# A hybrid decoder layer on one core: token sums moved to VectorE, first weight sums made earlier, weight slots moved, and another product order in the down projection

## The chip, the core and the metric

One core of a Trainium2 chip runs the whole layer in one launch. The metric is the device time of that launch in microseconds. The engines are named as in the profile: PE (TensorE), DVE (VectorE), ACT (ScalarE), POOL (GpSimd), and SP, which here only issues DMAs. POOL issues a few DMAs too. Every engine runs its instructions in the order in which they stand, and an instruction that waits holds up all behind it on that engine.

## The reference, cut to what matters

```python
u  = rmsnorm(x, attn_pre_norm)                    # x: 1024 tokens x 1024, float32
mix = concat(latent attention, HGRN2 recurrence)  # from one input projection
h  = x + rmsnorm(mix @ w_out, attn_post_norm)
z  = rmsnorm(h, ffn_pre_norm)
ff = silu(z @ w_gate) * (z @ w_up)                # width 2816
out = h + rmsnorm(ff @ w_down, ffn_post_norm)
```

## The kernel before, in words

The tokens lie in 8 blocks of 128. Three stages matter here: w_out (blocks y, some 540 to 618 us in the profile), gate and up (618 to 1073), and down (1073 to the end).

**Float32 by three products.** Each operand is split into a high part (a cast to fp32r on ACT) and a low part (a subtraction on DVE). A product is high x high, high x low and low x high, accumulated in PSUM.

**Seven products in place of eight.** Gate, up and down use a Strassen form (Winograd's variant): both operands are cut into 2 x 2 blocks, sums of blocks are made, and seven block products p1 to p7 replace eight. Of the tokens, b11, b21 and b22 are blocks and t1 to t4 are sums (`t1`, `t2` per token block at L965 to L971, `t3` at L1159, `t4` at L1164). Of each weight pair m (11 pairs of gate and of up columns, so m = 0 to 21, even for gate, odd for up) `w_sums` (L1002) makes three sums and L1019 a fourth. Of the down weights `wd_sum` (L1087) makes four sums on POOL, which go to `wb_d` in HBM. `ff_out` (L1068) makes four sums of the result of a pair on POOL and stores seven blocks to `fa_d`; down reads both back.

**w_out.** For each block t the mixed values are split (`mh` on ACT, `ml` on DVE L831), PE runs 48 matmuls, then z(t-2) is transposed (`z_t`, `zt` at L962), and `post_y`, `post_z` make h and z on DVE and ACT. The block's x comes by a DMA on SP into one of two buffers (L927), free once block t-2 has been transposed. DVE needs x at L939 and writes the normed block at L948. Up to block 6 a scheduler sets the order, from there on the order is that of the program text (`manual_schedule`, L1116).

**Gate and up.** The table `seq` (L984 to L987) lists 154 pairs (m, p), each a product of 12 matmuls of 128x512 at L1041. `w_prep` (L1009) splits a weight block into one of eight slots, six products ahead: slots 0 to 3 are the tile `wvg` (pool `gen`, on the right side of SBUF), slots 4 to 7 the tile `wvx` (pool `fqp`, on the left). The weights come through the tile `w4`; `w_load` is issued when the last block of the pair two before has been split. `post` (L1044) reads PSUM. The first 20 or so products stand in an order of their own, mixed with the last two token blocks' transposes (L1181 to L1228). For m below 4 the weight sums are on POOL, and so are the token sums t3 and t4.

**Down.** 77 steps (p, i), seven products of 11 steps; a step is one 512 KB load into one of four buffers `dgen` (`d_load`, L1237), one split (`d_prep`, L1242: a cast on ACT, a subtraction on DVE of 128x1024) and 12 matmuls (L1352), 3 for each of four token blocks j. The last steps of each product are run block by block (three steps, six in the last product), so that the results of block 0 leave PSUM (`d_post`, L1321) while the others are still at work. In the last product p3 each block's result goes through a square with a sum (ACT), a root (`rms_s`) and the output (`half`, `out_t`).

Of the kernel before, what the change touches and what calls it, by code (L numbers as in the profile page):

```python
# [85 lines left out]
def hymba_block(ctx: ExitStack, tc: tile.TileContext, a: dict, out: bass.AP):  # L86
# [53 lines left out]
    def rms_s(ss, name):  # L140
# [861 lines left out]
    def w_sums(m, E_):  # L1002
        a11, a12, a21, a22 = (ws_[m][:, j, :] for j in range(4))
        s1 = ffq["s1", m % 2]
        E_.tensor_tensor(s1, a21, a22, op=ALU.add)
        E_.tensor_tensor(a21, a11, a21, op=ALU.subtract)
        E_.tensor_tensor(a11, s1, a11, op=ALU.subtract)  # L1007

    def w_prep(n):  # L1009
# [57 lines left out]

    def ff_out(i):  # L1068
# [31 lines left out]
    for t in range(NT - 1):  # L1100
# [47 lines left out]
    wvx = fqp.tile([P, 2 * (NS - 4), 512], F32R, name="wvx")  # L1148
    wv += [wvx[:, 2 * j:2 * j + 2, :] for j in range(NS - 4)]
# [35 lines left out]
    for m in range(2):  # L1185
        w_sums(m, G)
# [61 lines left out]
    dgen, d_slots = None, [wvg[:, 4:8], wvx[:, 0:4], wvx[:, 4:8]]  # L1248

    for n in range(9, len(seq)):  # L1250
# [213 lines left out]
```

## Time and profile before

| | us |
|---|---|
| median of 3 runs | 1303.67 (1303.16 to 1304.64) |
| the profiled execution's own time | 1302.41 |
| its span | 1299.90 |
| PE busy | 1243.6 |
| DVE busy | 893.2 |
| ACT busy | 559.1 |
| POOL busy | 344.0 |

The profiled execution is one run of the same program; what lies around its span is 2.51 us. PE is busy for 96% of the span, so the stretches in which it is not, and those in which its granted clock (PEclk; 1.00 is 2.4 GHz, 0.50 is 1.2 GHz) is low, are what to look for. Matmuls overlap: one lasts 390 ns, but the next starts some 230 ns after it.

### The profile page before, as it was taken

How to read it: one execution, taken by the hardware profiler on the slowest of the kernel's cores; microseconds unless marked ns; L12 is line 12 of the kernel's file. 1: busy time of each engine (PE TensorE's matmuls, PEld its weight loads, DVE VectorE, ACT ScalarE, POOL GpSimd, SP SyncE). 2: the span in 40 equal slices, each digit the busy share in tenths (PEclk: the TensorE clock that was granted, in tenths of full speed). 3: DMA queues.
4: the chain of work that ended last, by engine and by line, in shares of the span. 5: the costliest groups of instructions: out<-in, count | busy, mean ns of one | idle time of the engine just before them, and what ended most of it. 6: DMA issues, size and time to landing. Idle time of an engine off the chain costs nothing.

```text
span 1299.9 us, 18112 instructions
## 1 busy us (share of the span) xinstructions
PE 1243.6 (96%) x6436; PEld 1034.1 (80%) x6436; DVE 893.2 (69%) x1786; ACT 559.1 (43%) x1202; POOL 344.0 (26%) x401
## 2 busy tenths in 40 slices
PE   8999999999999998999789999999999998999996
PEld 6987787898788887888567888888888887888885
DVE  6837657543888989677977777667677664555578
ACT  6424334336867766444432222333222333444352
POOL 1015433411232334000565523233323221000000
PEclk8999999999999998999889999999999998999998
DMA  8330100101000002225025453444353447755765
GB/s 281 108 114 18 49 27 10 35 5 65 19 7 8 33 1 81 87 101 186 33 82 182 173 186 120 156 170 164 135 187 130 154 161 256 242 183 180 257 200 189
DMA packets 61386, 155.20 MB, mean 119 GB/s; under 512 B 7153, under 2 KB 8561, under 8 KB 61297
## 3 DMA queue, kind: packets, MB, share of 16 engines
q1 hardware_dynamic: 60192, 150.38, 33.7%
q0 software_dynamic: 1104, 3.67, 0.8%
q8 instruction: 51, 0.84, 0.3%
q14 instruction: 39, 0.31, 0.1%
HBM read 112.87 MB, written 41.16 MB: 118 GB/s over the span
## 4 chain that ended last, share of the span: by engine, by line
PE 74%; DVE 13%; ACT 4%; issue 3%; DMA 3%; POOL 2%; SPq 0%; DVEq 0%; ACTq 0%; POOLq 0%
PE g_B L1041 8%; PE g_E L1041 8%; PE g_A L1041 8%; PE dy_B L1352 5%; PE g_C L1041 4%; PE dy_A L1352 4%; PE dy_C L1352 2%; PE dy_E L1352 2%; PE ao L768 2%; PE lv L437 2%; PE y L96 2%; PE y L95 2%; PE y L94 2%; PE lat_ps L96 1%; DVE s L737 1%
## 5 line engine op out<-in xcount | busy, mean ns | idle before, releaser
L1245 DVE TENSOR_TENSOR dhl<-dgen,dhl 128x1024 fp32r<-128x1024 f32 x74 | 89.3, 1223 | 73.8 <-ACT dhl L1244 73.5
L1244 ACT CAST dhl<-dgen 128x1024 fp32r<-128x1024 f32 x74 | 76.5, 1050 | 99.4 <-PE dy_B L1352 32.0
L1022 ACT CAST wvx<-w 128x512 fp32r<-128x512 f32 x64 | 39.0, 617 | 105.7 <-DVE w L1007 46.1
L1023 DVE TENSOR_TENSOR wvg<-w,wvg 128x512 fp32r<-128x512 f32 x64 | 58.8, 920 | 31.3 <-ACT wvg L1022 31.2
L1022 ACT CAST wvg<-w 128x512 fp32r<-128x512 f32 x64 | 39.1, 617 | 94.2 <-DVE w L1019 40.6
L1023 DVE TENSOR_TENSOR wvx<-w,wvx 128x512 fp32r<-128x512 f32 x64 | 53.1, 830 | 33.4 <-ACT wvx L1022 33.3
L738 ACT ACTIVATE pe<-s,nm 128x128 f32<-128x128 f32 (+3 forms) x64 | 47.7, 746 | 40.0 <-DVE nm L737 24.0
L1073 POOL TENSOR_TENSOR fq_p<-fq_u,fq_p 128x512 f32<-128x512 f32 x11 | 19.0, 1731 | 173.3 <-DVE fq_u L1066 173.3
L1352 PE MATMUL dy_B<-dhl 128*128 128x512 f32 x264 | 60.2, 389 | 0.0
L1352 PE MATMUL dy_E<-dhl 128*128 128x512 f32 x264 | 60.2, 389 | 0.0
L1352 PE MATMUL dy_A<-dhl 128*128 128x512 f32 x228 | 55.5, 405 | 3.3 <-ACT dhl L1244 2.7
L1352 PEld LDWEIGHTS dy_E<-dhl 128*128 128x128 f32 x264 | 49.5, 188 | 10.3
L1352 PEld LDWEIGHTS dy_B<-dhl 128*128 128x128 f32 x264 | 49.5, 188 | 10.3
L1313 POOL DMA_DIRECT2D out_dram<-ot x8 | 4.4, 548 | 195.5 <-DVE ot L1312 195.1
L1352 PEld LDWEIGHTS dy_A<-dhl 128*128 128x128 f32 x228 | 44.7, 197 | 13.7 <-ACT dhl L1244 3.1
L759 DVE TENSOR_TENSOR ptl<-pt,pth 128x512 fp32r<-128x512 f32 (+2 forms) x96 | 49.9, 552 | 4.4 <-ACT pth L758 3.6
L755 PE MATMUL pt<-cc,pe 128*128 128x128 f32 x288 | 44.9, 277 | 6.2 <-DVE oT L774 5.5
L737 DVE CUSTOM_DVE_ANT_0 s<-mbuf,s 128x128 f32<-128x128 bf16 (+6 forms) x56 | 41.9, 749 | 7.2 <-PE s L728 6.3
L758 ACT CAST pth<-pt 128x512 fp32r<-128x512 f32 (+2 forms) x96 | 43.6, 483 | 6.1 <-PE pt L755 6.0
L458 POOL TENSOR_TENSOR kk<-kk,tt 128x128 f32<-128x128 f32 (+1 forms) x88 | 40.8, 493 | 14.1 <-PE lv L453 14.1
L755 PEld LDWEIGHTS pt<-cc,pe 128*128 128x128 f32 x288 | 34.1, 142 | 12.2 <-DVE oT L774 7.2
L1054 DVE TENSOR_TENSOR fq_u<-g_B,fq_p 128x512 f32<-128x512 f32 x22 | 15.2, 691 | 34.5 <-PE g_B L1041 23.0
(475 smaller groups left out, 3906.3 us busy)
## 6 DMA issues: line engine op xcount, KB each, us to landing
dgen<-fa_p SPq DMA_DIRECT2D x77, 256.0 KB, 3.8
w<-in_w_gate_dram SPq DMA_DIRECT2D x22, 512.0 KB, 4.2
w<-in_w_up_dram SPq DMA_DIRECT2D x22, 512.0 KB, 5.1
wdr<-in_w_down_dram SPq DMA_DIRECT2D x22, 512.0 KB, 6.3
wb_d<-wdr SPq DMA_DIRECT2D x22, 512.0 KB, 6.4
fa_p<-fq_u SPq DMA_DIRECT2D x44, 256.0 KB, 2.0
dgen<-wb_d SPq DMA_DIRECT2D x44, 256.0 KB, 4.2
dgen<-in_w_down_dram SPq DMA_DIRECT2D x33, 256.0 KB, 4.1
```

The costliest lines, as they stand in the source:

```text
L458: E_.tensor_tensor(v_, v_, pick(tg, 2 * n * j + to_, t_[c_:]), op=ALU.mult)
L737: V.tensor_tensor_reduce(sv, mv, sv, op0=ALU.add, op1=ALU.min, scale=1.0, scalar=3e38, accum_out=nm)
L738: A.activation(pv, sv, AF.Exp, bias=nm, scale=-1.0, accum_out=zz[:, NT * h + qb:NT * h + qb + 1])
L755: T.transpose(tps[:, j, :], pe[:, (k0 + j) * P:(k0 + j + 1) * P], ident)
L758: A.copy(th[o], tps[:, 0:n, :])
L759: V.tensor_tensor(tl[o], tps[:, 0:n, :], f32(th[o]), op=ALU.subtract)
L1022: A.copy(wh, src)
L1023: V.tensor_tensor(wl, src, f32(wh), op=ALU.subtract)
L1041: T.matmul(o, l_[:, k_], r_[:, k, :], start=first and k == 0 and i == 0, stop=k == 3 and i == 2, skip_group_check=True)
L1244: A.copy(hl[:, 0, :], raw)
L1245: V.tensor_tensor(hl[:, 1, :], raw, f32(hl[:, 0, :]), op=ALU.subtract)
L1352: T.matmul(dq[bank[p]][j], hl[:, lh, j_], hl[:, rh, 512:1024], start=first and x_ == 0, stop=i == NP - 1 and x_ == 2, skip_group_check=True)
```

## The change

- The token sums t3 and t4 run on DVE; t3 in one piece after the last block, t4 in six steps after products 9 to 14.
- The weight sums of m = 0 to 3 are made on POOL during w_out, from block 0 to 3 on, one m for each (`w_pre`), and stored to `ws_d` in HBM. `w_load` reads them back. The blocks that p1 and p2 need come through `w_early` for all four.
- The eight weight slots are two tiles `wva`, `wvb` in `gen` on the right side; `w4` has a pool of its own on the left, takes its first loads after w_out, and serves down's loads as well (so `dgen` is `w4`).
- The order of p3 and p4 for m = 0, 1, the places of the last two blocks' work, of `wd_load`, `wd_sum`, `wd_store` and of `ff_out`'s last four stores (`ff_store`) are others.
- Down's products run as p1, p2, p6, p5, p3, p7, p4 in place of p1, p6, p2, p5, p7, p4, p3; the last product's last eight steps run block by block in place of six. Loads 4 to 6 of down are issued in the last gate and up products. A part of the root's sum is made earlier.

```diff
-DN_END = 6
+DN_END = 8
+T4_AT = 9
+PRE = 4
+DN_PRODUCTS = ("p1", "p2", "p6", "p5", "p3", "p7", "p4")
...
-    seq += [(m, p) for p in ("p5", "p7") for m in range(2)]
-    seq += [(m, p) for m in range(2) for p in ("p3", "p4")]
+    seq += [(m, p) for p in ("p5", "p7", "p3", "p4") for m in range(2)]
...
+            SP.dma_start(wq[:, j, :], ws_d[m, j] if m < PRE else w_of[m % 2][m // 2 + NP * j])
+        if m < PRE:
+            SP.dma_start(ffq["s1", m % 2], w_of[m % 2][m // 2 + NP][:, 512:1024])
...
+    def w_pre(m):
+        pre_ = [wr.tile([P, D], F32, name=f"wp{m}_{j}", tag="wr") for j in range(2)]
+        for j in range(2):
+            SP.dma_start(pre_[j], w_of[m % 2][m // 2 + NP * j])
+        (a11, a12), (a21, a22) = ([x_[:, d_] for d_ in halves] for x_ in pre_)
+        G.tensor_tensor(a22, a21, a22, op=ALU.add)
+        G.tensor_tensor(a21, a11, a21, op=ALU.subtract)
+        G.tensor_tensor(a11, a22, a11, op=ALU.subtract)
+        G.tensor_tensor(a12, a12, a11, op=ALU.subtract)
+        for j in range(2):
+            SP.dma_start(ws_d[m, j], pre_[j])
...
-        if p == "p6" and m > 1:
-            w_sums(m, G if m < 4 else V)
-        if p == "p3":
+        if p == "p6" and m >= PRE:
+            w_sums(m)
+        if p == "p3" and m >= PRE:
             V.tensor_tensor(a12, a12, a11, op=ALU.subtract)
...
         post_y(t)
         post_z(t)
+        if t < PRE:
+            w_pre(t)
...
-    w4[0] = gen.tile([P, 4, 1024], F32, name="w4", tag="gen")
-    wvg = gen.tile([P, 8, 512], F32R, name="wvg", tag="gen")
+    for x_ in "ab":
+        wg_ = gen.tile([P, 8, 512], F32R, name=f"wv{x_}", tag="gen")
...
-    wvx = fqp.tile([P, 2 * (NS - 4), 512], F32R, name="wvx")
...
+    def t3_sum():
+            V.tensor_tensor(zr["t1"], zr["t1"] if i else zr["t2"], f32(x_), op=ALU.subtract)
+    def t4_step(x):
+            V.tensor_tensor(t4r[j], f32(zv["b21"][i][:, j_, :]), t4r[j] if i else zr["t2"][:, j_, :],
+                            op=ALU.add if i else ALU.subtract)
...
-    for m in range(2):
-        w_sums(m, G)
     product(0)
...
             d_prep(e_ // 2, d_slots[e_ // 2].rearrange("p (x a) c -> p x (a c)", x=2))
+            d_load(e_ // 2 + 4)
...
+        if first:
+            V.tensor_tensor(ssy[:, o_:o_ + 1], ssy[:, o_:o_ + 1], eps, op=ALU.add)
...
-            (SP if t < 4 else G).dma_start(out[t][:, d_], ot[:, d_])
+            (G if t < 4 else SP).dma_start(out[t][:, d_], ot[:, d_])
```

Three places show how instructions moved.

SP's queue in w_out, around the loads of x for blocks 4 and 5. Before (`xr_6554`, `xr_6657` are x of blocks 4 and 5, `h_3` to `h_5` stores of h):

```order
L940 DMA h_d<-h_3_6453 128x1024
L927 DMA xr_6554<-in_x_dram 128x1024
L940 DMA h_d<-h_4_6556 128x1024
L927 DMA xr_6657<-in_x_dram 128x1024
L940 DMA h_d<-h_5_6659 128x1024
```

After (`xr_6595`, `xr_6698` are x of blocks 4 and 5; `wp` a pair whose sums POOL makes, `ws_d` its store, `we` an early load):

```order
L1007 DMA wp_0_6514<-in_w_up_dram 128x1024
L947 DMA h_d<-h_3_6484 128x1024
L1007 DMA wp_1_6515<-in_w_up_dram 128x1024
L931 DMA xr_6595<-in_x_dram 128x1024
L1014 DMA ws_d<-wp_1_6515 128x1024
L1014 DMA ws_d<-wp_0_6514 128x1024
L1020 DMA we_6846<-in_w_gate_dram 128x1024
L947 DMA h_d<-h_4_6597 128x1024
L1020 DMA we_6848<-in_w_up_dram 128x1024
L931 DMA xr_6698<-in_x_dram 128x1024
```

The x of block 5 now stands behind two stores that wait for POOL's sums of m = 3, and behind two loads that wait for these stores.

DVE from the last block's t1 split to the t3 split in gate and up. Before (`wvg`, `wvx` the weight slots, `zr_t` the raw token sums):

```order
L953 TENSOR_TENSOR z_t1l<-zr_t_6164,z_t1h 128x4x128
L1023 TENSOR_TENSOR wvx<-w_6803,wvx 128x512
L1066 TENSOR_TENSOR fq_c_6905<-g_A,fq_c_6905 128x512
L1023 TENSOR_TENSOR wvg<-we_7056,wvg 128x512
L1023 TENSOR_TENSOR wvg<-w_6803,wvg 128x512
L1023 TENSOR_TENSOR wvg<-s_0_6900,wvg 128x512
L1052 TENSOR_TENSOR fq_u_6903<-g_B,fq_p_6902 128x512
L953 TENSOR_TENSOR z_t3l<-zr_t_6164,z_t3h 128x2048
```

After:

```order
L960 TENSOR_TENSOR z_t1l<-zr_t_6165,z_t1h 128x4x128
L1047 TENSOR_TENSOR wvb<-w_6947,wvb 128x512
L1090 TENSOR_TENSOR fq_c_6962<-g_A,fq_c_6962 128x512
L1047 TENSOR_TENSOR wva<-we_6911,wva 128x512
L1203 TENSOR_TENSOR zr_t_6165<-zr_t_6166,z_b11h 128x2048
L1203 TENSOR_TENSOR zr_t_6165<-zr_t_6165,z_b11l 128x2048
L1047 TENSOR_TENSOR wva<-w_6947,wva 128x512
L960 TENSOR_TENSOR z_t3l<-zr_t_6165,z_t3h 128x2048
L1047 TENSOR_TENSOR wva<-w_6947,wva 128x512
L1076 TENSOR_TENSOR fq_u_6960<-g_B,fq_p_6959 128x512
```

The two t3 sums stand on DVE ahead of the splits for products 9 and 10; before, POOL made them.

SP's queue at the end of gate and up. Before (`fa_p` from `fq`: stores of a pair's result; `dgen` loads of down's steps, each in two halves, here step 4's):

```order
L1078 DMA fa_p_74<-fq_p_6906 128x512
L1078 DMA fa_p_75<-fq_u_6903 128x512
L1078 DMA fa_p_72<-fq_u_6908 128x512
L1078 DMA fa_p_77<-fq_u_6907 128x512
L1239 DMA dgen<-fa_p_71 128x512
L1240 DMA dgen<-in_w_down_dram 128x512
L1294 DMA fpost<-in_ffn_post_dram 128x1024
```

After (`w_6947` is `w4`; the first four rows load steps 5 and 6, step 4's stand earlier; `wb_d` from `wdr` stores down's weight sums):

```order
L1274 DMA w_6947<-fa_p_71 128x512
L1275 DMA w_6947<-in_w_down_dram 128x512
L1274 DMA w_6947<-fa_p_71 128x512
L1275 DMA w_6947<-in_w_down_dram 128x512
L1126 DMA wb_d<-wdr_0_9781 128x1024
L1126 DMA wb_d<-wdr_1_9782 128x1024
L1098 DMA fa_p_71<-fq_c_6962 128x512
L1098 DMA fa_p_73<-fq_u_6961 128x512
L1098 DMA fa_p_76<-fq_p_6959 128x512
L1108 DMA fa_p_74<-fq_p_6963 128x512
L1108 DMA fa_p_75<-fq_u_6960 128x512
L1108 DMA fa_p_72<-fq_u_6965 128x512
```

Loads 4 to 6 moved ahead of the last pair's stores; the first load behind them, after one of `fpost`, is now step 7's.

## Rows read from the trace of the kernel before

**Rows 1.** The page's first part: busy time of each engine.
```profile
PE 1243.6 (96%) x6436; PEld 1034.1 (80%) x6436; DVE 893.2 (69%) x1786; ACT 559.1 (43%) x1202; POOL 344.0 (26%) x401
```
**Rows 2.** Stretches: length, each engine's busy time (instructions), PEclk, DMA share, GB/s.
```profile
618.30:692.80 74.50, 60.77 (x234) 47.62 (x233) 60.65 (x68) 27.29 (x44) 45.63 (x23) 0.86 0.17 57
...
1073.40:1110.30 36.90, 33.61 (x134) 26.85 (x133) 17.23 (x15) 14.05 (x15) 6.03 (x4) 0.91 0.79 270
...
625.00:630.00 5.00, 4.43 (x12) 3.26 (x11) 4.56 (x12) 1.12 (x5) 1.00 (x1) 0.50 0.00 2
```
**Rows 3.** PE's longest wait from 605 to 720 us: total, times, longest.
```profile
PE g_E L1041 <- DVE fq_p L1055: 5.6, 1, 5.6
```
**Rows 4.** PE in order of time: start, length, [idle before].
```profile
618.23 0.39 PE L1041 MATMUL g_A<-z_b11h,wvg 128*128 128x512 f32 x1
...
623.56 1.97 PE L962 MATMUL zt<-cc,xr 128*128 128x128 f32 x8 [2.42 <-DVE xr L948]
...
630.75 0.39 PE L1041 MATMUL g_A<-z_b21h,wvg 128*128 128x512 f32 x1
...
692.78 0.40 PE L1041 MATMUL g_B<-z_t2h,wvg 128*128 128x512 f32 x1
...
705.70 0.39 PE L1041 MATMUL g_C<-z_t4h,wvx 128*128 128x512 f32 x1
```
**Rows 5.** POOL and DVE in order of time, in the same stretch.
```profile
615.78 1.74 POOL L1005 TENSOR_TENSOR s<-w 128x512 f32<-128x512 f32 x1 [93.18 <-DVE rr_z L135]
...
616.29 1.25 DVE L136 TENSOR_TENSOR rt_z<-rr_z 128x1 f32<-128x1 f32 x1
...
619.24 0.68 DVE L968 TENSOR_TENSOR zr_t<-zt,z_b11h 128x512 f32<-128x512 f32 x1
...
637.22 1.75 DVE L953 TENSOR_TENSOR z_t1l<-zr_t,z_t1h 128x1536 fp32r<-128x1536 f32 x1
...
639.60 3.48 DVE L968 TENSOR_TENSOR zr_t<-zr_t,z_b11l 128x512 f32<-128x512 f32 x1
```
**Rows 6.** w_out: DVE and SP by time; DMA issues, median us to landing.
```profile
538.55 2.35 DVE L157 TENSOR_TENSOR wol<-wo_r,woh 128x1024 fp32r<-128x1024 f32 x2
...
582.79 0.33 SPq L927 DMA_DIRECT2D xr<-in_x_dram  x1
...
594.67 0.33 SPq L927 DMA_DIRECT2D xr<-in_x_dram  x1
...
606.09 0.69 DVE L831 TENSOR_TENSOR ml<-mixa,mh 128x512 fp32r<-128x512 f32 x1 [1.82 <-PE zt L962]
...
h_d<-h SPq DMA_DIRECT2D x6, 512.0 KB, 2.6
...
w<-in_w_gate_dram SPq DMA_DIRECT2D x2, 512.0 KB, 4.1
```
**Rows 7.** PE: first matmuls of four products, two with each slot tile.
```profile
1051.34 0.39 PE L1041 MATMUL g_E<-z_b22h,wvg 128*128 128x512 f32 x1
...
1054.06 0.39 PE L1041 MATMUL g_A<-z_b11h,wvg 128*128 128x512 f32 x1
...
1059.55 0.39 PE L1041 MATMUL g_A<-z_b21h,wvx 128*128 128x512 f32 x1
...
1062.35 0.39 PE L1041 MATMUL g_E<-z_t1h,wvx 128*128 128x512 f32 x1
```
**Rows 8.** Start of down: SP by time; then the chain of waits.
```profile
1081.74 0.38 SPq L1239 DMA_DIRECT2D dgen<-fa_p  x1
...
1110.28 29.92 PE dy_B L1352 x132
```
**Rows 9.** End of the span: PE and DVE by time; a stretch as in rows 2.
```profile
1259.72 30.08 PE L1352 MATMUL dy_E<-dhl 128*128 128x512 f32 x132
...
1292.31 0.68 DVE L1342 TENSOR_TENSOR d_u<-dy_E,d_u 128x512 f32<-128x512 f32 x1
...
1284.00:1288.00 4.00, 4.00 (x19) 3.34 (x18) 3.56 (x11) 1.02 (x3) 0.00 (x0) 1.00 0.48 188
```

More of the change, by code (lines that the diff above doesn't have):

```diff
@@ L1066, in post @@
                 V.tensor_tensor(sl, o if p == "p2" else own(done), sl, op=ALU.mult)
+    wd_at = {**{2 * i + 3: i for i in range(NP - 2)}, 2 * NP - 2: NP - 2, 2 * NP - 1: NP - 1}
     def ff_out(i):
@@ L1117, in hymba_block @@
     ms.__enter__()
-    w4[0] = gen.tile([P, 4, 1024], F32, name="w4", tag="gen")
-    wvg = gen.tile([P, 8, 512], F32R, name="wvg", tag="gen")
-    wv += [wvg[:, 2 * j:2 * j + 2, :] for j in range(4)]
-    for m in range(2):
-        w_load(m)
+    for x_ in "ab":
+        wg_ = gen.tile([P, 8, 512], F32R, name=f"wv{x_}", tag="gen")
+        wv += [wg_[:, 2 * j:2 * j + 2, :] for j in range(4)]
+        wvt.append(wg_)
+    w_early(0)
+    w_early(1)
+    w_prep(0)
+    w_prep(2)
+    w_early(2)
+    w_prep(1)
+    w_prep(4)
+    x_get(last)
     mix_mm(last, order, (0,))
     post_y(last, (0,))
-    w_early(2)
-    for n in range(4):
-        w_prep(n)
     z_t(last - 2, sm)
+    w_prep(3)
+    w_prep(5)
+    w_early(3)
     mix_mm(last, order, (1,))
@@ L1134, in hymba_block @@
     ps.close()
+    w4_st = ExitStack()
+    w4p = pool(w4_st, "w4p")
+    w4[0] = w4p.tile([P, 4, 1024], F32, name="w4")
     f_st = ExitStack()
@@ L1139, in hymba_block @@
         ffq["s1", i] = fqp.tile([P, 512], F32, name=f"s1_{i}")
+    for m in range(2):
+        w_load(m)
     def ff_tiles(p_, par):
@@ L1228, in hymba_block @@
     w_prep(14)
-    steps = [(p, i) for p in PRODUCTS for i in range(NP)]
+    steps = [(p, i) for p in DN_PRODUCTS for i in range(NP)]
     dv = {}
@@ L1246, in d_prep @@
         dv[n] = hl
-    dgen, d_slots = None, [wvg[:, 4:8], wvx[:, 0:4], wvx[:, 4:8]]
+    dgen, d_slots = w4[0], [wvt[0][:, 4:8], wvt[1][:, 0:4], wvt[1][:, 4:8]]
     for n in range(9, len(seq)):
@@ L1294, in hymba_block, with half @@
     SP.dma_start(fpost, a["ffn_post"].partition_broadcast(P))
-    p1_, u2_, u3_ = (dp.tile([P, 4, 512], F32, name=f"d_{x_}") for x_ in ("p1", "u2", "u3"))
-    dq, ots, hrs = {}, {}, {}
-    def half(t, d, src):
+    p1_, u2_, u3_, p5_ = (dp.tile([P, 4, 512], F32, name=f"d_{x_}") for x_ in ("p1", "u2", "u3", "p5"))
+    dbank = {"p1": "A", "p2": "A", "p6": "B", "p7": "B", "p5": "E", "p3": "E", "p4": "C"}
+    dq, otg, ots, hrs = {}, {}, {}, {}
+    def half(t, d, src, first):
         d_ = halves[d]
-        if t not in ots:
-            ots[t] = dp.tile([P, D], F32, name=f"ot{t}", tag="ot", bufs=8)
+        if t // 4 not in otg:
+            otg[t // 4] = gen.tile([P, 4, 1024], F32, name=f"ot{t // 4}", tag="gen")
+        ots[t] = otg[t // 4][:, t % 4, :]
         sq = dp.tile([P, 512], BF16, name=f"sr{t}_{d}", tag="sr", bufs=1)
@@ L1351, in d_mm @@
         for x_, (lh, rh) in enumerate(((0, 0), (0, 1), (1, 0))):
-            T.matmul(dq[bank[p]][j], hl[:, lh, j_], hl[:, rh, 512:1024], start=first and x_ == 0,
+            T.matmul(dq[dbank[p]][j], hl[:, lh, j_], hl[:, rh, 512:1024], start=first and x_ == 0,
                      stop=i == NP - 1 and x_ == 2, skip_group_check=True)
```

150 lines of the change are left out of this document (77 added, 73 removed).

## The prediction

> **What bounds the kernel now.** I read the busy times first: PE works for 1243.6 of 1299.9 us [rows 1], so time can only come from PE's waits, its clock and the pitch of its matmuls. Then the stretches: the start of gate and up (PE busy 60.77 of 74.50, PEclk 0.86), the start of down (33.61 of 36.90, PEclk 0.91) [rows 2], and the end, where PE is done before the span is. Then PE's waits in the first of these [rows 3], and PE, POOL and DVE there in order of time.
>
> *Start of gate and up.* Product 0 begins at 618.23, product 18 at 692.78, product 21 at 705.70 [rows 4]. A product takes 2.72 or 2.80 us in the undisturbed part [rows 7]; with 2.74 and 0.8 for each of two transposes, 18 products are worth 50.9 us and took 74.55, the next three 8.2 and took 12.92. So 23.6 + 4.7 = 28.3 us are lost. Half is waiting and half is clock: PE waited 2.42 for block 6's transpose, and product 2, due at 620.98 + 0.8 + 2.74 = 624.5, began at 630.75 [rows 4], since PEclk was 0.50 after the wait [rows 2]. The longest wait, 5.6 [rows 3], is for DVE while POOL makes t4 and the weight sums of m = 2. POOL also slows DVE: an op of 128x1 took 1.25 us, ending with a POOL op, and a 128x512 one with both inputs in SBUF 3.48; one with an input in PSUM took 0.68 beside a busy POOL [rows 5].
>
> *Start of down.* The first product has 132 matmuls, 29.92 us when nothing waits (the next one's row), but ran from 1073.4 to 1110.28 [rows 2, 8]: 6.9 us lost. Step 4's load stood in SP's queue behind the last pair's stores and left at 1081.74 [rows 8].
>
> *End.* The last product's matmuls end at 1259.89 + 29.92 = 1289.81 (issue times; the row is [rows 9]), but DVE takes block 3's result at 1292.31, 2.5 us late. A block's 18 matmuls give it 4.1 us, and it is busy for 3.56 of 4.00 [rows 9], with short waits for ACT between, so it cannot make up what it was behind at the first block.
>
> **The change part by part.** The sum is made against the profiled execution (1302.41, 1.3 under the median) and taken off the median, since it is a difference.
>
> *1. Weight sums in w_out.* It takes 12 POOL ops off the start of gate and up and puts 16 of 1.3 to 1.74 us [rows 5] beside w_out, and adds 8 loads and 8 stores of 512 KB to SP's queue. One pair's cycle is 4 x 1.7 for POOL, 2.6 for the store, 4.1 for the next load [rows 6] and some 0.7 of issuing: 14.2 us. A block of w_out is 11.88 (two x loads, 582.79 and 594.67), so the cycles fall behind. If the first pair's sums end at 552 (its buffers come free at 540.9 [rows 6]; then a load and POOL), the fourth's end at 552 + 42.6 = 594.6, its store lands at 597.2, and the x of block 5, queued behind two more loads, leaves at 598.6, not 594.67 [rows 6]. DVE then has it 4 us late. Behind it on DVE stand the norm of block 5, three weight splits (1.8 us) and the split `ml` of block 7, which was ready at 606.8 and would be at 610.8. PE needs it 12 matmuls into block 7, which starts behind the transpose that frees `ml`'s buffer, so at 606.3 + 2.7 = 609.0: it waits 1.8 us. Bounds: nothing, if the cycle is 13 us; about 11 with clock lost, if POOL's ops take 2.2 (the cycle is 16.2, x leaves 9.9 late).
>
> On what POOL costs DVE the Trainium skill (SBUF — State Buffer, Who interferes with whom) says that a VectorE op with two SBUF inputs and a GpSimd op that reads SBUF shut each other out for the whole instruction, and one with an SBUF and a PSUM input doesn't. [Rows 5] agree with both halves. By it alone, 16 moved ops of 1.3 us block DVE by up to 21 us within the 47 us of four blocks; what of that reaches PE is then a second way to the delay above.
>
> *2. Token sums on DVE, order of the start.* DVE gets 2 x 2.3 us for t3 (128x1536 takes 1.75 [rows 5], scaled by size), 4 x 1.2 and 2 x 1.2 for t4: 11.9 us, and loses four sums of 0.68 and all slowing by POOL. Laying after's DVE order end to end with these durations from 610.8 on: x of block 6 is normed at 622.8, when PE (1.8 late) ends product 0: no wait where 2.42 stood. Block 7 is normed at 633.1; PE asks at 631.8: 1.3 of wait. The splits of t2 and of slot 7 end at 642.4, PE asks at 642.1; then the two t3 sums (4.6 us) stand ahead of product 9's split, ready at 649.1 while PE asks at 647.9: 1.2. Products 10 and 16 cost 0.3 and 0.2, with t4's six steps between the splits, which run six products ahead. `w4` is read back at some 624 to 630, before slot 7's split. Together with part 1: 1.8 + 1.3 + 0.3 + 1.2 + 0.3 + 0.2 = 5.1 us of waits, and I add 1.5 for clock (the wait of 2.42 came with 3.8 of it, [rows 4]). 28.3 - 6.6 = 21.7 gained. Bounds: 28.3 (no wait left); and 8, if all 11.9 us of DVE work show on PE with as much again lost by half clock as in [rows 4], where 2.42 of wait became 6.2.
>
> *3. Slots on the right side.* Products with `wvg` begin 2.72 us apart, with `wvx` 2.80 (1051.34 to 1054.06, 1059.55 to 1062.35 [rows 7]). From product 21 on 67 use `wvx`, of which ten with t2 (left side as well) take 2.76 from either tile: 57 x 0.08 = 4.5; I take 4.2. Bounds 0 (if the place isn't the cause) and 5.
>
> Here the skill speaks against a gain: the same section says that PE never waits on anyone for SBUF, and knows only contention of DVE with GpSimd. By that the slot's place is worth 0. The rows differ by 3% whatever its cause; I go with them and keep 0 as a rival.
>
> *4. Start of down.* Loads 4 to 6 leave after the splits of steps 0 to 2, some 12 us earlier. Late next is step 7, behind the stores: it leaves at about 1081.7, lands 4.1 later, is split by 1089, and PE asks at 1073.4 + 7 x 2.72 = 1092.4. Gain 6.9; bounds 0 and 6.9.
>
> *5. Order of down, end.* PE showed no wait between down's products, so the order is worth 0; the copies that p2 and p3 now wait for are block by block ahead of PE. Eight steps per block give DVE 24 x 0.227 = 5.4 us, so block 3's chain begins at PE's end: 2.5 gained, and 0.2 for the sum made earlier. Step 76's split waits for the buffer of the last product's third step and stands behind a block's sums on DVE and ACT; laid out, it is some 0.5 us late. I take 2.3; bounds 0 and 2.7.
>
> Sum: 21.7 + 4.2 + 6.9 + 2.3 = 35.1. 1303.67 - 35.1 = 1268.6, or 1269.
>
> **The rivals.**
> - *Forecast*, 1269, own range 1262 to 1276: all four parts give about this. 50%.
> - *w_out pays.* SP's queue as in part 1, but at 6 us late and more: PE waits about 4 at block 7 and half clock follows, some 8 beyond my 1.8: 1277. For it: the cycle of 14.2 is longer than 11.88, and three more DMAs of 512 KB share the time of x's. Against: 2.2 us of slack and PSUM inputs that POOL doesn't hold. 18%.
> - *DVE bounds the start.* From 622 to 650 my layout leaves DVE no idle time; any op late by more than I take falls on PE, each wait with clock behind it: part 2 gives 12, not 21.7: 1278. 15%.
> - *The slot's place is worth nothing*: 1273. For it: the skill's rule; against: [rows 7]. 12%.
> - *Slower.* The same queue, where each pair's cycle is so long that x comes some 37 us late: the x of block 5 leaves 3 cycles - 38.7 us late, PE loses that less the 2.2 between 606.8 and 609.0, and it takes some 35 to eat all gains. It decides from a cycle of 25.3, POOL ops of 4.5 us each; the row beside a busy DVE is 1.74 [rows 5]. At a cycle of 26.5 us the gains are passed by 3.6: 1307. 3%.
> - That the change does not do what it says is left 2%: the orders show each move.
>
> **How the numbers follow.** 1269 is the likeliest. The upper ends: w_out and DVE together, 1286; the lower: all 28.3 + 5 + 6.9 + 2.7 = 42.9 gained, 1261. Range 1259 to 1287. 0.2% (2.6 us) is what a measurement of this kernel tells from no change; only the slower rival and a pile of several others reach it. Faster 0.95, same 0.02, slower 0.03.
>
> **What would show it.** Right: product 0 to product 21 in some 64 us where 87.5 stood; no POOL op between 605 and 660; no DVE op of 128x1 over 0.3 there; PE's down products 29.9 each, the first too; products all at 2.72 apart from t2's; DVE's last result within 0.3 us of PE's end. Wrong: a wait of PE on `ml` or `h` between 570 and 610 (part 1), on `wva` or `zt` over 2 us after it (part 2), products at 2.80 with `wvb` (part 3), PE waiting on `dhl` at steps 4 to 8 or at step 76 (parts 4, 5). Wrong by more than the range: PEclk of 0.5 in w_out.

## The result, and the profile after

The changed kernel takes 1285.52 us (median of 4 runs, 1281.86 to 1285.88) beside 1303.41 of the kernel before: a ratio of 0.9856, 95% interval 0.9836 to 0.9876. So 16 to 21 us are gained, half of the 35.1 forecast, and the time lies at the upper end of the range. The profiled execution took 1285.21, its span is 1283.40.

The page's busy times, for [rows 1]. PE has 12.8 us less of busy time, which is half clock and slow pitch gone, since the matmuls are the same:

```profile
PE 1230.8 (96%) x6436; PEld 1024.2 (80%) x6436; DVE 905.6 (71%) x1790; ACT 560.4 (44%) x1206; POOL 328.5 (26%) x395
```

To see where the time went I cut both spans at the same five places of the program: the transposes of block 0 in w_out (the first `zt` behind 550 us), the first matmul of product 0, that of product 21, down's first, the last product's first, and the end. Columns as in [rows 2]: stretch, length, then busy time of PE, PEld, DVE, ACT and POOL, PEclk, DMA share, GB/s. First before, then after.

```profile
557.98:618.23 60.25, 60.25 (x289) 50.09 (x288) 44.06 (x105) 26.62 (x65) 2.37 (x2) 1.00 0.41 145
618.23:705.70 87.47, 70.94 (x270) 55.48 (x268) 70.86 (x76) 30.09 (x49) 55.93 (x29) 0.86 0.25 84
705.70:1073.42 367.72, 367.72 (x1598) 299.38 (x1596) 257.89 (x339) 108.60 (x188) 117.99 (x76) 1.00 0.44 160
1073.42:1259.72 186.30, 183.01 (x794) 150.55 (x793) 98.35 (x93) 77.44 (x89) 6.03 (x4) 0.98 0.67 223
1259.72:1299.90 40.18, 30.08 (x133) 24.59 (x131) 33.51 (x84) 13.65 (x30) 4.38 (x8) 0.90 0.55 185
```

```profile
556.70:625.43 68.73, 61.95 (x289) 49.75 (x288) 54.32 (x111) 28.59 (x69) 19.13 (x12) 1.00 0.57 203
625.43:691.13 65.70, 61.19 (x269) 48.52 (x268) 56.24 (x76) 29.29 (x48) 6.15 (x4) 1.00 0.37 124
691.13:1056.19 365.06, 364.02 (x1598) 299.34 (x1596) 270.13 (x338) 109.21 (x189) 126.78 (x80) 1.00 0.47 167
1056.19:1242.32 186.13, 182.18 (x793) 149.63 (x794) 107.35 (x122) 80.57 (x97) 13.53 (x13) 0.99 0.72 239
1242.32:1283.40 41.08, 32.26 (x133) 25.64 (x131) 28.03 (x56) 11.72 (x25) 0.00 (x0) 0.90 0.32 116
```

| stage | before | after | gain | forecast |
|---|---|---|---|---|
| w_out, from block 0's transposes | 60.25 | 68.73 | -8.5 | -1.8 |
| products 0 to 20 | 87.47 | 65.70 | 21.8 | 23.5 (21.7 with the 1.8 taken off) |
| rest of gate and up | 367.72 | 365.06 | 2.7 | 4.2 |
| down's first six products | 186.30 | 186.13 | 0.2 | 6.9 |
| last product to the end | 40.18 | 41.08 | -0.9 | 2.3 |

With 1.3 from ahead of all that (557.98 to 556.70) these make the 16.5 between the spans. The start of gate and up came out nearly as forecast, at full clock (PEclk 1.00 where 0.86 stood). Every stage gave less than forecast, three of them by 3 us or more: w_out, the start of down and the end. PE's waits in these parts of the changed kernel (total, times, longest) say what for; [rows 3] had 5.6 in one.

```profile
PE y L99 <- DVE ml L835: 4.0, 2, 2.7
PE dy_A L1396 <- ACT d_p L1367: 3.1, 1, 3.1
PE g_E L1065 <- DVE fq_p L1079: 2.0, 2, 1.4
PE y L97 <- ACT mh L834: 1.6, 1, 1.6
...
PE y L97 <- DVE rr_y L139: 1.1, 1, 1.1
PE dy_A L1396 <- DVE dhl L1280: 0.8, 2, 0.7
PE dy_C L1396 <- ACT dhl L1279: 0.8, 1, 0.8
...
PE dy_C L1396 <- DVE dhl L1280: 0.8, 1, 0.8
```

*w_out.* Two stalls. The first, 2.66, is at 566, where PE waits for `ml`. DVE makes `ml` behind small ops of the norms, and of these some end only when POOL's sum of the second pair (m = 1) beside them ends, as in these rows; the second is POOL's:

```profile
562.05 1.27 DVE L152 TENSOR_TENSOR rv_y<-ssy 128x1 f32<-128x1 f32 x1
```
```profile
563.38 2.31 POOL L1010 TENSOR_TENSOR wp<-wp,wp 128x512 f32<-128x512 f32 x1
```
```profile
564.50 1.21 DVE L140 TENSOR_TENSOR rt_y<-rr_y 128x1 f32<-128x1 f32 x1
565.63 0.68 DVE L835 TENSOR_TENSOR ml<-mixa,mh 128x512 fp32r<-128x512 f32 x1
```

Before, such 128x1 ops took 0.15 each in this place, POOL had nothing to do, and the same `ml` stood 4.3 earlier in its block:

```profile
561.24 0.15 DVE L148 TENSOR_TENSOR rv_y<-ssy 128x1 f32<-128x1 f32 x1
...
562.63 0.68 DVE L831 TENSOR_TENSOR ml<-mixa,mh 128x512 fp32r<-128x512 f32 x1
```

The second stall is in block 7 (1.60, 1.36 and 1.11 of the list). SP's row [rows 6] had x at 594.67; now it goes out at 601.39, behind the fourth pair's stores, which wait for POOL, and the loads behind these. DVE waits 3.21 for it:

```profile
594.95 3.39 SPq L1014 DMA_DIRECT2D ws_d<-wp  x2
...
601.39 0.44 SPq L931 DMA_DIRECT2D xr<-in_x_dram  x1
```
```profile
607.15 1.28 DVE L946 SCALAR_TENSOR_TENSOR h<-h,rr_y,xr 128x1024 f32<-128x1024 f32 x1 [3.21 <-DMA xr<-in_x_dram]
```

*Rest of gate and up*, for [rows 7]: products begin 2.72 apart with either slot tile, except t2's and the one behind it, b21's, with 2.77.

```profile
1036.50 0.39 PE L1065 MATMUL g_A<-z_b11h,wva 128*128 128x512 f32 x1
...
1039.22 0.40 PE L1065 MATMUL g_B<-z_t2h,wvb 128*128 128x512 f32 x1
...
1041.99 0.40 PE L1065 MATMUL g_A<-z_b21h,wvb 128*128 128x512 f32 x1
...
1044.76 0.39 PE L1065 MATMUL g_E<-z_t1h,wvb 128*128 128x512 f32 x1
```

*Start of down*, for [rows 8]. Step 7's load leaves 12.2 us after down's first matmul (1056.19), not 8.3 as the prediction had it from step 4's of [rows 8], and PE waits 0.67 for its split. Most of the 3.9 lies with POOL: the stores ahead of this load wait for POOL's four sums of the last pair, and these end 11.3 after down's first matmul, not 7.9 as before. Now they run beside DVE's splits of steps 3 to 6, which the earlier loads have made possible, and take some 2.2 each; before, DVE had no such split then, and the last three took 1.3. The last sum before, then the last sum and the splits after:

```profile
1080.02 1.28 POOL L1076 TENSOR_TENSOR fq_u<-fq_u,fq_u 128x512 f32<-128x512 f32 x1
```
```profile
1065.30 2.15 POOL L1102 TENSOR_TENSOR fq_u<-fq_u,fq_u 128x512 f32<-128x512 f32 x1
```
```profile
1058.39 7.92 DVE L1280 TENSOR_TENSOR dhl<-w,dhl 128x1024 fp32r<-128x1024 f32 x4
```

The larger wait is 3.12: p2 adds onto p1's PSUM banks, so its first matmul needs the copy of p1 (`d_p`), and this stands on ACT behind the casts of two late loads, at 1088.08 and 1089.41. Half clock follows (PEclk 0.57 in the 4 us behind the wait): 132 matmuls take 31.80 where [rows 9] have 30.08.

```profile
1068.37 0.41 SPq L1274 DMA_DIRECT2D w<-fa_p  x1
```
```profile
1088.08 1.04 ACT L1279 CAST dhl<-w 128x1024 fp32r<-128x1024 f32 x1 [2.87 <-DMA w<-in_w_down_dram]
1089.41 1.04 ACT L1279 CAST dhl<-w 128x1024 fp32r<-128x1024 f32 x1 [0.29 <-DMA w<-in_w_down_dram]
1090.36 2.04 ACT L1367 COPY d_p<-dy_A 128x512 f32<-128x512 f32 x4
```
```profile
1076.41 4.42 PE L1396 MATMUL dy_A<-dhl 128*128 128x512 f32 x18 [0.67 <-DVE dhl L1280]
...
1090.99 31.80 PE L1396 MATMUL dy_A<-dhl 128*128 128x512 f32 x132 [3.12 <-ACT d_p L1367]
```

*End*, for [rows 9]. The last result is taken 0.03 after PE's end (1257.45 + 18.68 = 1276.13), as forecast. But PE itself came late: two waits of 0.8 for the split of step 76, and 4 us of PEclk 0.57 behind them.

```profile
1256.19 0.50 PE L1396 MATMUL dy_C<-dhl 128*128 128x512 f32 x1 [0.80 <-ACT dhl L1279]
1257.45 18.68 PE L1396 MATMUL dy_C<-dhl 128*128 128x512 f32 x74 [0.76 <-DVE dhl L1280]
```
```profile
1276.17 0.69 DVE L1386 TENSOR_TENSOR d_u<-dy_C,d_u 128x512 f32<-128x512 f32 x1 [1.43 <-PE dy_C L1396]
```
```profile
1258.00:1262.00 4.00, 4.00 (x12) 3.12 (x11) 3.38 (x10) 1.74 (x5) 0.00 (x0) 0.57 0.00 0
```

### The profile page after: what moved, and what is told of

The parts are those of the page before. It is cut to its first block, busy times and chain, and to the rows that moved or that the text cites. A ratio compares the mean times of both kernels' runs of the same rounds, so it can differ in the third digit from the quotient of the medians.

```text
span 1283.4 us, 18152 instructions
## 1 busy us (share of the span) xinstructions
PE 1230.8 (96%) x6436; PEld 1024.2 (80%) x6436; DVE 905.6 (71%) x1790; ACT 560.4 (44%) x1206; POOL 328.5 (26%) x395
## 4 chain that ended last, share of the span: by engine, by line
PE 69%; DVE 13%; DMA 6%; ACT 5%; issue 3%; POOL 3%; SPq 0%; DVEq 0%; ACTq 0%; POOLq 0%
PE g_B L1065 9%; PE g_E L1065 8%; PE g_A L1065 8%; PE dy_B L1396 5%; PE dy_E L1396 5%; PE g_C L1065 4%; PE dy_A L1396 2%; PE ao L772 2%; PE lv L441 2%; PE dy_C L1396 1%; DVE s L741 1%; PE lat_ps L99 1%; PE lat_ps L97 1%; PE lat_ps L98 1%; DMA w<-in_w_down_dram 1%
## 5 line engine op out<-in xcount | busy, mean ns | idle before, releaser
L1280 DVE TENSOR_TENSOR dhl<-w,dhl 128x1024 fp32r<-128x1024 f32 x74 | 92.3, 1267 | 65.0 <-ACT dhl L1279 64.7
L1279 ACT CAST dhl<-w 128x1024 fp32r<-128x1024 f32 x74 | 76.2, 1048 | 100.7 <-DMA w<-in_w_down_dram 29.7
L1046 ACT CAST wva<-w 128x512 fp32r<-128x512 f32 x62 | 37.8, 617 | 92.6 <-DVE w L1027 41.3
L1047 DVE TENSOR_TENSOR wva<-w,wva 128x512 fp32r<-128x512 f32 x62 | 55.5, 895 | 31.5 <-ACT wva L1046 31.3
L1046 ACT CAST wvb<-w 128x512 fp32r<-128x512 f32 x62 | 37.5, 616 | 90.4 <-DVE w L1027 49.7
L1047 DVE TENSOR_TENSOR wvb<-w,wvb 128x512 fp32r<-128x512 f32 x62 | 52.2, 843 | 32.9 <-ACT wvb L1046 32.8
L1119 POOL TENSOR_TENSOR wdr<-wdr 128x512 f32<-128x512 f32 x11 | 16.4, 1488 | 198.2 <-DMA wdr<-in_w_down_dram 184.7
```

The source lines that it names most:

```text
L1046: A.copy(wh, src)
L1047: V.tensor_tensor(wl, src, f32(wh), op=ALU.subtract)
L1279: A.copy(hl[:, 0, :], raw)
L1280: V.tensor_tensor(hl[:, 1, :], raw, f32(hl[:, 0, :]), op=ALU.subtract)
```

## The experiments

All start from the changed kernel. Stages are named as in the table above; what the expectations call block 2's transpose is the same cut, the transposes of block 0, made while block 2 is at work. Ratios are to runs of the kernel before on the same chip, with their 95% intervals; the changed kernel's is 0.9856 (0.9836 to 0.9876). The intervals of e3, e4 and e5 overlap this one, so the time alone doesn't show that each of them is faster; what each edit does is read from its stage. e2 to e5 came out 0.1 to 1.6 under the times expected: stages that their edits don't touch were shorter too.

**e1: the sums of the first pairs on DVE, in gate and up.** (Before, POOL made them there.)

```diff
-PRE = 4
+PRE = 0
```

> The changed kernel with no pair's sums made in w_out: VectorE makes those of all pairs, three subtractions and additions at the p6 slot and one at p3. Theory (the sums in w_out, by GpSimd's lock and by the loads behind their stores, cost what w_out lost): product 0 of gate and up begins at about 617 instead of 625.4, and the waits on ml and mh go. In the start of gate and up VectorE gets 16 ops of 0.61 more, and has only some 5 us idle there, so product 0 to 21 takes 70 to 75 instead of 65.7. Time 1281 to 1288, near the 1285.5. Rival (w_out lost to the early weight splits of the first six slots, which stay): product 0 still at 623 to 625, time 1290 to 1295.

Measured: 1292.78 us, ratio 0.9922 (0.9895 to 0.9949). w_out takes 60.29, product 0 begins at 618.61, no wait on `ml` or `mh`: all of the 8.4 is the price of `w_pre`. Products 0 to 20 take 80.94, 15.2 more, beyond the 75 expected: 16 ops of 0.61 are 9.8 us of DVE, and the rest came with them (PEclk 0.94). So making the sums in w_out is better than this, and the time is slower than the range named. The rival is out. The sums on POOL at the start of gate and up, as before, with the token sums on DVE, were not run.

**e2: the transfers alone.** It leaves out the sums, so these pairs are loaded and stored raw.

```diff
-        (a11, a12), (a21, a22) = ([x_[:, d_] for d_ in halves] for x_ in pre_)
-        G.tensor_tensor(a22, a21, a22, op=ALU.add)
-        G.tensor_tensor(a21, a11, a21, op=ALU.subtract)
-        G.tensor_tensor(a11, a22, a11, op=ALU.subtract)
-        G.tensor_tensor(a12, a12, a11, op=ALU.subtract)
```

> Leaves out the sums of the first four pairs: the pairs are loaded and stored raw during w_out, so their slots hold raw weights. DMAs as in the changed kernel, no GpSimd op in w_out. Theory (GpSimd's lock on VectorE and the loads of x that queue behind stores waiting for GpSimd make the loss): the wait of 2.66 at 569 goes, x of block 5 leaves before 598 instead of 601.4, product 0 begins at 617 to 619: time 1277 to 1279. Rival (the 8 MB more of transfers slow the loads of x by themselves): the waits of block 7 stay at 3 us or more, product 0 at 622 or later.

Measured: 1276.9, ratio 0.9805 (0.9782 to 0.9828). No stall at all in w_out; the stage is as long as before, at 215 GB/s where e1 has 111:

```profile
560.09:620.38 60.29, 60.29 (x289) 50.08 (x288) 46.16 (x111) 28.93 (x68) 0.00 (x0) 1.00 0.62 215
```

The 8 MB cost nothing here. What costs is POOL: its ops and what waits for them.

**e3: x from ACT's queue.**

```diff
-            SP.dma_start(xts[t], a["x"][t])
+            A.dma_start(xts[t], a["x"][t])
```

> The loads of x in w_out are issued by ScalarE instead of SP, all else as in the changed kernel. Theory (two causes: GpSimd's lock makes the 2.66 at 569, the queue on SP makes the 4.1 of waits in block 7): x of block 5 leaves before 597, the waits of block 7 go, that of 2.66 stays; product 0 at 620 to 621, time 1280 to 1282. Rival 1 (the lock alone makes both): product 0 stays at 624 to 625.5. Rival 2 (the queue alone): product 0 at 617.

Measured: 1278.91, ratio 0.9820 (0.9794 to 0.9846). The waits of block 7 are gone; the stall at 569 stays, 3.65 here with half clock behind it, and is all that is left of w_out's loss (65.68 against 60.25). So there are two causes, as the theory had it; product 0 at 623.89 is later than expected, since this stall was larger. In e4, where x is on SP, it was 3.64.

```profile
568.86 0.80 PE L99 MATMUL y<-woacs,ml 128*128 128x512 f32 x1 [3.65 <-DVE ml L835]
```

How the loss is shared between the two stalls differs from execution to execution. e4 to e7 run w_out unchanged, with x on SP: from block 0's to block 3's transposes they lost 5.3 to 6.8 us (the changed kernel's profile 3.0), from there to product 0 only 0.2 to 2.6 (5.5 there), in all 6.8 to 7.9 (8.5 there). With x on ACT's queue (e3, e8, e9, e10) nothing was lost in the second part. So the queue is a cause, but its 5.5 in the profile was a dear case, and e3's edit is worth some 1 to 3 us.

**e4: p6 between p1 and p2.**

```diff
-DN_PRODUCTS = ("p1", "p2", "p6", "p5", "p3", "p7", "p4")
+DN_PRODUCTS = ("p1", "p6", "p2", "p5", "p3", "p7", "p4")
```

> Down's products in the order p1, p6, p2, p5, p3, p7, p4: p6, in PSUM banks of its own, stands between p1 and p2. Theory (p2, which adds onto p1's banks, waits 3.12 for ScalarE's copy of p1, which stands behind splits of late loads; 1.8 of half clock follows): both go, the first two products take 61 to 62 instead of 66.45; time 1280 to 1281.5. Rival (the late loads are what limits, and the copy only stands where they would): PE waits on dhl at steps 11 to 16 instead, the first two products take 65 or more, time 1284 to 1286.

Measured: 1279.29, ratio 0.9822 (0.9796 to 0.9848). The first two products take 31.40 + 29.92 = 61.3; the wait for the copy is gone and none on `dhl` at steps 11 to 16 stands in its place (that of step 7, 0.77 here, stays), so the rival is out.

```profile
1078.52 11.24 PE L1396 MATMUL dy_A<-dhl 128*128 128x512 f32 x47 [0.77 <-DVE dhl L1280]
1089.60 30.08 PE L1396 MATMUL dy_B<-dhl 128*128 128x512 f32 x132
```

The gain of 5.1 is measured against one execution. In the profiles of e2, e3, e5, e6 and e7, which run this code unchanged, the first two products took 62.9 to 64.0 (copy wait 1.8 to 2.3), in e1 67.3: typical is 1.6 to 2.6.

**e5: seven kept-back steps.**

```diff
-DN_END = 8
+DN_END = 7
```

> The last product keeps back 7 steps for its block-by-block end instead of 8, all else as in the changed kernel. Theory (with 8, step 76 is needed 12.9 us into the product, when its split, behind block sums on VectorE and ScalarE, is not made: two waits of 0.8 and, in some executions, 1.9 of half clock): needed 2.04 later, it is ready; no wait of PE on dhl, the last product takes 29.9 to 30.2, and from its start to the end of the span 37.3 to 37.6 instead of 41.08 (39.6 to 39.8 where the clock held). VectorE's share of a block, 4.0, still fits in the 4.8 of 21 matmuls. Time 1281 to 1283.5. Rival (with shorter ends VectorE is late after the last matmul, or the split is late by more than 2): 39 or more, time as the changed kernel's.

Measured: 1279.44, ratio 0.9827 (0.9804 to 0.9851). No wait in the last product, 30.17 for its 132 matmuls, 37.4 from its start to the end. As the theory had it. In the executions with eight steps this stage took 39.4 to 39.8 (e1, e3, e4, e7) or 41.1 to 41.7 (the changed kernel, e2, e6), with waits of 1.6 to 2.2.

**e6: token sums on POOL.**

```diff
 def t3_sum():
-            V.tensor_tensor(zr["t1"], zr["t1"] if i else zr["t2"], f32(x_), op=ALU.subtract)
+            G.tensor_tensor(zr["t1"], zr["t1"] if i else zr["t2"], f32(x_), op=ALU.subtract)
...
 def t4_step(x):
-            V.tensor_tensor(t4r[j], f32(zv["b21"][i][:, j_, :]), t4r[j] if i else zr["t2"][:, j_, :],
+            G.tensor_tensor(t4r[j], f32(zv["b21"][i][:, j_, :]), t4r[j] if i else zr["t2"][:, j_, :],
...
-        V.tensor_tensor(l_, t4r[j], f32(h_), op=ALU.subtract)
+        G.tensor_tensor(l_, t4r[j], f32(h_), op=ALU.subtract)
```

> The sums t3 and t4 of the tokens at the start of gate and up, and the last step of t4's split, go back to GpSimd, the order of the program and the pre-made weight sums as in the changed kernel. Theory (the engine mattered: an op of 128x512 takes GpSimd 1.3 to 2.3, where VectorE takes 0.6, and the lock slows VectorE's other work): t4 is late, PE waits for z_t4 or for wva behind locked ops, product 0 to 21 takes 74 to 82 instead of 65.7, time 1294 to 1303. Rival (with the weight sums gone from the start, GpSimd would have had the time for the token sums, and the gain is the weight sums'): 65 to 69, time 1285 to 1289.

Measured: 1292.39, ratio 0.9921 (0.9887 to 0.9954), products 0 to 20 in 74.84. The theory holds at its lower end (the time is 2 under the range). The rows show how: DVE's split of a weight block, 0.68 elsewhere, lasts as long as POOL's sum beside it.

```profile
645.23 4.92 POOL L1203 TENSOR_TENSOR zr_t<-zr_t,z_b11h 128x2048 f32<-128x2048 f32 x1 [48.79 <-DVE z_t1l L960]
```
```profile
646.21 4.50 DVE L1047 TENSOR_TENSOR wva<-we,wva 128x512 fp32r<-128x512 f32 x1
650.63 5.05 DVE L1047 TENSOR_TENSOR wva<-w,wva 128x512 fp32r<-128x512 f32 x1
```

The Trainium skill (SBUF — State Buffer, Who interferes with whom) says that such a pair shuts each other out for the whole instruction; these rows agree. Of the 21.8 gained at this start, then, 9.1 hang on the engine of the token sums (against POOL) and 15.2 on the weight sums being made earlier (against DVE, e1); the two overlap.

**e7: tiles swapped.**

```diff
-    zv = {q: [zp.tile([P, 4, 512], F32R, name=f"z_{q}{x_}") for x_ in "hl"] for q in ("b11", "b21", "b22")}
+    zv = {q: [zp.tile([P, 4, 512], F32R, name=f"z_{q}{x_}") for x_ in "hl"] for q in ("b21", "b11", "b22")}
...
-    zv["t2"] = [fqp.tile([P, 4, 512], F32R, name=f"z_t2{x_}") for x_ in "hl"]
+    zv["t1"] = [fqp.tile([P, 4, 512], F32R, name=f"z_t1{x_}") for x_ in "hl"]
...
-    for q in ("t1", "t3"):
+    for q in ("t2", "t3"):
```

> In the changed kernel, the tiles of t1 and t2 change places in SBUF, and so do those of b11 and b21; nothing else. There, products of t2 and b21 begin 2.76 to 2.77 after one another, all others 2.72. Theory (the place of the operand sets the pitch of the matmuls): now t1 and b11 show 2.76 to 2.77, t2 and b21 2.72; time as the changed kernel's, within 2. Rival (it is what these two products do, their banks or their neighbours): t2 and b21 stay at 2.76 to 2.77.

Measured: 1284.62 (two runs), ratio 0.9859 (0.9828 to 0.9890). Half of it as the theory had it. Now t1's product takes 2.76 and t2's 2.72, so the 2.76 belongs to the place on the left side. But b11, in b21's old place, takes 2.72, and so does b21; the other slow one is now t3's, the product behind t1's:

```profile
1044.15 0.39 PE L1065 MATMUL g_A<-z_b21h,wvb 128*128 128x512 f32 x1
...
1046.87 0.40 PE L1065 MATMUL g_E<-z_t1h,wvb 128*128 128x512 f32 x1
...
1049.63 0.40 PE L1065 MATMUL g_B<-z_t3h,wvb 128*128 128x512 f32 x1
...
1052.40 0.39 PE L1065 MATMUL g_C<-z_t4h,wva 128*128 128x512 f32 x1
```

So a moving operand in this place on the left slows its own product and the next one by 0.05. Why the next one stays open. The Trainium skill (the same section) has it that PE never waits on anyone for SBUF; with the place as the only edit, the pitch moved.

**e8: three edits together** (those of e3, e4 and e5).

> Three edits on the changed kernel together: x loaded from ScalarE's queue in w_out, down's products in the order p1, p6, p2, p5, p3, p7, p4, and 7 steps kept back in the last product. Theory (the three stalls are in stages of their own, and add): block 2's transpose to product 0 in 65.7 instead of 68.73, product 0 to 21 in 66, start of down to the last product 181.0 instead of 186.13, its start to the end 37.3 instead of 41.08: 12 us under the changed kernel, 1273 to 1275 (beside a run of the kernel before of 1303). Rival (the three share a cause, late loads, and what one gives the next takes): 1277 to 1280.

Measured: 1275.84 (1274.90 to 1278.08), ratio 0.9794 (0.9776 to 0.9812): faster than both kernels, 1 over the range expected. The stages are 65.53, 66.46, 365.11, 181.01 and 37.4, the four that were named met within 0.5: the stalls are separate and add. By the ratios the time is some 8 under the changed kernel's, not 12. The 12 had been taken from one profile of the changed kernel, whose start of down and end were dear beside other executions of the same code (e4, e5); and in e8's profile what lies ahead of the five stages took 1.6 longer (558.26 against 556.70), without an edit there.

**e9 to e12: the stall left in w_out** (all with e8's edits). First, other blocks for the pairs, in e9 three of them as here, in e10 four (`PRE = 4`, and `4: 3` added to the table):

```diff
-PRE = 4
+PRE = 3
+PRE_AT = {0: 0, 2: 1, 3: 2}
...
-        if t < PRE:
-            w_pre(t)
+        if t in PRE_AT:
+            w_pre(PRE_AT[t])
```

> The three edits of the run before, and three pairs pre-made instead of four, in blocks 0, 2 and 3 of w_out: no GpSimd op between 560 and 570, where two blocks' norms fill VectorE. The fourth pair's sums go back to VectorE, 4 ops of 0.61. Theory (only the pair of block 1 meets a VectorE without slack; the others hide): block 2's transpose to product 0 in 60.3 to 60.6, where 65.53 stood, product 0 to 21 in 66 to 69: 2 to 5 under the three edits' 1275.8, that is 1271 to 1274. Rival (the first pair, at 546 to 553, is what carries VectorE late into block 2): a wait on ml of 2 or more stays, and the time is 1275 to 1278.

> As the run with pairs in blocks 0, 2 and 3, with the fourth pair pre-made in block 4, at about 603 to 609. Theory: block 2's transpose to block 7 without a wait as there, but the raw loads for the first six slots take their two buffers from this pair, and leave only behind its stores, at about 611: PE waits 2 to 4 for wva at product 0 or for z behind it, and VectorE is saved 2.4 later: 1270 to 1275, no better than three pairs. Rival (the first slots' loads have that slack): product 0 as with three pairs, and 2 under them.

Measured: e9 1282.92, ratio 0.9846 (0.9825 to 0.9868); e10 1276.38, ratio 0.9789 (0.9766 to 0.9811). Neither tests the theory: the second pair's ops still ran at 560.38 and 561.41, since up to block 6 the scheduler starts a pair as soon as its buffers are free, wherever it stands in the program. The stalls stayed (5.3 and 3.2). e9 prices the fourth pair: without it products 0 to 20 take 70.58, 4.1 more than in e8.

Then a dependency that holds the pair back: two DVE copies of 128x1 into its buffers, before its loads, from the normed block 1 in e11 (below) and from `h1s[t]`, its h, in e12.

```diff
+            if gate is not None:
+                V.tensor_copy(pre_[j][:, 0:1], gate[:, 0:1])
             SP.dma_start(pre_[j], w_of[m % 2][m // 2 + NP * j])
...
-            w_pre(t)
+            w_pre(t, xts[t] if t == 1 else None)
```

> The three edits, four pairs pre-made, and the loads of the second pair wait for the norm of block 1 (two VectorE copies of 128x1 from its result into the pair's buffers, which the loads then overwrite). Its GpSimd ops then stand at about 568 to 575 instead of 560 to 567. Theory (the stall of 3.6 and its half clock come from this pair's lock on VectorE while it norms blocks 1 and 2; at 568 and later VectorE has slack): no wait on ml of over 1, block 2's transpose to product 0 in 60.3 to 62, all else as with the three edits: 1271 to 1273. Rival 1 (the sums cost the same wherever they stand in w_out): the wait moves to 575 to 585, 65 to 66 stay, time 1275 to 1277. Rival 2 (the later pairs come too late for the first slots): the wait shows on wva at products 0 to 2.

> As the run before, but the second pair's loads wait only for h of block 1, some 4 us earlier: its GpSimd ops at about 566 to 573, the fourth pair's at 595 to 601, the first slots' loads out by about 605. Theory (two limits: the second pair not before the norms of blocks 1 and 2, the fourth early enough that ScalarE's casts of the first slots are done before it is asked for block 7's mh): both waits small, block 2's transpose to product 0 in 60.5 to 62.5 where the three edits took 65.53 and the later pair 68.54; 1270.5 to 1273.5 (beside 1303 of the kernel before). Rival (there is no gap between the limits): a wait of 2 or more with half clock at one of the two places, 64 or more, 1275 or more.

Measured: e11 1278.17, ratio 0.9806 (0.9788 to 0.9824); e12 1275.93, ratio 0.9784 (0.9763 to 0.9805). In e11 the pair ran at 571 to 577, and the block that took 17.14 in e8 took 13.13 (11.88 without a stall): the theory holds, this pair's place makes that stall. But the fourth pair then ends at 605, the first slots' loads leave behind its stores, and ACT, in order, casts `mh` of block 7 behind their casts: PE waits 3.12 + 1.17 with half clock (stage 68.54). A second wait took the place of the first, by another path than the rival named (`mh`, not `wva`).

```profile
614.36 0.62 ACT L1048 CAST wva<-we 128x512 fp32r<-128x512 f32 x1 [1.30 <-DMA we<-in_w_up_dram]
...
614.88 0.61 ACT L834 CAST mh<-mixa 128x512 fp32r<-128x512 f32 x1
```

e12 has both waits, smaller (1.2 on `ml` at 566; 1.4 on `mh` and 1.7 on `ml` in block 7; stage 67.36): its rival was right on the stage, no gap between the two limits was found. e8, e10 and e12 cannot be told apart. The work of four pairs on POOL in w_out cost 5 to 8 us wherever it was put here (stages of 65.24 to 68.54 against 60.25).

## Why the prediction came out as it did

The direction was right, and so was the start of gate and up as the largest gain and in its size; the sum was 17 too large (19 against the span).

- *Part 1, w_out, failed in two ways.* The larger one had been left at nothing: POOL's lock on DVE. The prediction priced it (16 x 1.3 us) and called it a second way to the same delay. It was a delay of its own, in another block: the second pair meets the norms of blocks 1 and 2, where DVE has little slack (e2, e11). It cost 3.0 in the profile and 5.3 to 6.8 in e4 to e7. It also escaped the sign named for it, a wait between 570 and 610: it ended at 566. The queue was the right mechanism, and here mis-sized: the pairs' cycle, put at 14.2, was 17.5, 15.1 and 14.2 from pair to pair, so the x of block 5 left at 601.39 and not 598.6, and block 7 lost 5.5 and not 1.8. In e4 to e7 it lost 0.2 to 2.6, about what was forecast.
- *Part 2* was right: 21.8 against 23.5. Products 0 to 20 took 65.70 where "some 64" was named, waits 4.5, the largest 1.4, and none of them brought half clock, for which 1.5 had been added. e1 and e6 show that the gain needs both moves.
- *Part 3* was right in what it rests on: seven products take 5 x 2.72 + 2 x 2.77 = 19.14 after, 367.72 / 19 = 19.35 before, 19 times 0.21 is 4.1 (4.2 forecast). The rule of the Trainium skill (SBUF — State Buffer, Who interferes with whom), that PE never waits on anyone, by which this was worth nothing, did not settle it here: the 2.80 are gone. The 1.4 that two new waits cost in the same stage (0.65 on `fq_p`, 0.4 ahead of down, and what followed them) were not foreseen.
- *Part 4* failed at two steps. Step 7's load was given the time at which step 4's had left before; it left 3.9 later, since the splits that the earlier loads allow slow POOL's last sums, for which the stores ahead of it wait. And in "the copies that p2 and p3 now wait for are block by block ahead of PE", the copy's own length was weighed, not what stands ahead of it on ACT: casts that wait for these late loads. 4.0 of waits and 1.7 of half clock took what the earlier loads gave; some 0.9 more I cannot place. e4 shows that putting p2 right behind p1 cost 1.6 to 5.1, not 0.
- *Part 5* named the right wait, step 76's, and sized it 0.5; it was 1.6 to 2.2, and behind it PE lost another 0.5 (e1, e3, e4, e7) or 2.1 (the changed kernel, e2, e6). With seven steps (e5) the forecast gain of 2.3 came, and a little more: 40.18 to 37.4.

None of the rivals describes the whole. "w_out pays" is the nearest, in place and size (6.7 beyond the forecast, 8 named), though its path, the queue, was the smaller share in most executions. Two losses, 6.7 at the start of down and 3.2 at the end, came on top. The time lies within the range because the range had been widened for several rivals together; all five stages came out under their forecast.

## What to carry to other kernels

Before costing a wait at nothing because its producer is short, list what stands ahead of that producer on its in-order engine, and what that in turn waits for: here a copy of 0.6 us cost 3 behind casts of late loads, an x load cost up to 4 behind stores that waited for POOL. Work put on POOL beside DVE is paid for in DVE's small SBUF-only ops, each of which can last a whole POOL instruction, so it belongs beside a stretch where DVE reads PSUM or has slack. When a forecast is a sum of gains in separate stages, cut both spans at the same program points: five rows told which terms had failed, and single edits could then be read from their own stage, finer than from the time.

## What the runs showed of the hardware that was not expected

- The granted clock's answer to a wait differs between executions of the same code: the two waits of 0.8 at the end were followed by 4 us of PEclk 0.57 in the changed kernel's profile, in e3, behind the same two waits, PEclk was 1.00 (39.5 against 41.08 for the stage). The 2.66 at 566 cost no clock (PEclk 1.00 in the 4 us behind it), the 3.65 in e3 at the same place did (0.60).
- Twelve matmuls take 0.05 longer with the moving operand in the place tried on the left side of SBUF, and so do the next twelve (e7); with the weights on the left instead, 0.08 [rows 7]. That the weights' place is the cause rests on rows: no run moved the slots alone.
- The lock works both ways: at the start of down, where four of each run beside one another, POOL's sums took 2.2 and not 1.3, and DVE's splits, the first apart, 2.3 and not 1.22.
